# Adaptive-norm modulation vectors: row sums on VectorE from transposed weights instead of column sums closed by TensorE

## Chip, cores and metric

One core of one Trainium2 chip runs the whole program. The metric is the device time of one execution in microseconds (us); the time of a kernel is the median of several runs. The engines are named as in the profile: PE is TensorE (PEld its weight loads), DVE is VectorE, ACT is ScalarE, POOL is GpSimd, and SP issues most of the DMA transfers.

## The reference

Two layers over 256 tokens of width 2048: an RWKV-7 time mix with an MLP, then a chunked band attention with an MLP. Each sub-layer is modulated by vectors that come from the conditioning vector `c` alone:

```python
for layer in range(DEPTH):                      # DEPTH = 2, D = 2048
    mod = c @ w_ada[layer] + b_ada[layer]       # (1, D) @ (D, 6 * D)
    sh1, sc1, gt1, sh2, sc2, gt2 = jnp.split(mod, 6, axis=-1)
    if layer == N_A_LAYERS:
        sh_kv, sc_kv = jnp.split(c @ w_ada_kv + b_ada_kv, 2, axis=-1)
        ...
    h = modulate(rms_norm(x, g_mix[layer]), sh1, sc1)
    ...
    x = x + gt1[:, None, :] * y
    h = modulate(rms_norm(x, g_mlp[layer]), sh2, sc2)
    x = x + gt2[:, None, :] * sq_relu_mlp(h, w_up[layer], w_down[layer])
```

So there are 14 modulation vectors of 2048 numbers, each a product of `c` with a 2048x2048 matrix of 16 MB in fp32. The change concerns the last twelve of them, in the order in which the kernel makes them: gate, scale, shift and gate of layer 0, the two of the shared key and value projection, and the six of layer 1.

## The kernel before

Activations lie transposed: a tile has 128 channels on its partitions and the 256 tokens along the row. A vector over channels lies as `[128, 16]`, channel `128*k + p` at partition `p`, column `k`. Every dense product runs in a split form: a weight tile `raw` of 128x1024 (512 KB, 4 KB for each partition) is loaded by SP, ScalarE rounds it to `wH` (`halves`, L378), VectorE forms the rest `wL = raw - wH` (L381), and TensorE multiplies both (`proj2`, L412 and L413). `raw` has six buffers, `wH` and `wL` three each.

The stages follow each other: the opening (to about 190 us) makes the first two modulation vectors and the value projection; then the recurrence of layer 0, 16 pairs of heads in a software pipeline of slots, beside the dense projections for the next pairs (`layer_a`, to about 680 us); its output projection (`out_proj`); the first MLP (`mlp`, four quarters of 16 up and 16 down tiles); the shared key and value projections and attention (`attention`); its output projection; and the second MLP. The order of instructions on each engine is a scheduler's; the program text gives the dependencies.

The twelve later modulation vectors are made in small steps between other work. `ada_tiles` lists the weight tiles: for each vector two halves of 1024 output columns, for each half 16 tiles of 128 rows. `ada_load` loads the next one (as `raw`, or as `rada` out of a pool of its own during the MLPs and attention), and `ada_step` takes one tile: `acc += c[row of the partition] * tile` on VectorE (L452 for the first tile of a half, L454 for the other fifteen), with `acc` a tile of 128x1024. Who calls it: one step in three of four slots of the recurrence, `ada_tick` with one or two steps for each MLP tile, one or two steps for each projection in attention, and `ada_need`, which makes what is still missing of a vector just before its use.

After the sixteenth tile of a half, `acc` holds for each of 1024 columns 128 partial sums, one on each partition. `ada_sum` adds them on TensorE: for each of 8 blocks of 128 columns and each group of 32 columns a matmul with `acc` as the stationary operand and a column of ones as the moving one, which leaves the sums spread over partitions in PSUM (L476); VectorE adds the bias into the vector `mods[key]` (L480). `fin` runs the generator to its end at once, since `lazy` is never set. The profile shows each of these fp32 matmuls as two.

Of the kernel before, what the change touches and what calls it, by code (L numbers as in the profile page):

```python
# [329 lines left out]
class Body:  # L330
# [88 lines left out]

    def ada_src(self, layer, part):  # L420
        if layer == "kv":
            at, w = 2 * 96 + 16 * part, self.d["w_ada_kv"]
        else:
            at, w = 96 * layer + 16 * part, self.d["w_ada"][layer]
        return w[:, part * D:(part + 1) * D], self.bada[:, at:at + KT]

    def ada_tiles(self):
        for key in [(0, 2), (0, 4), (0, 3), (0, 5), ("kv", 1), ("kv", 0),
                    (1, 1), (1, 0), (1, 2), (1, 4), (1, 3), (1, 5)]:
            for half in range(KT // HK):  # L430
                for kt in range(KT):
                    yield key, half, kt

    def ada_load(self):
        tile_ = next(self.adas, None)
        if tile_ is not None:
            key, half, kt = tile_
            w, n_ = self.ada_src(*key)[0], HK * P
            raw = self.raw(w[kt * P:(kt + 1) * P, half * n_:(half + 1) * n_], ada=True)
            self.ada_q.append((key, half, kt, raw))  # L440
        return tile_ is not None

    def ada_step(self):
        nc = self.nc
        if not (self.ada_q or self.ada_load()):
            return
        key, half, kt, raw = self.ada_q.popleft()
        ck = self.ct[:, kt:kt + 1]
        if kt == 0:
            self.fin(HK)  # L450
            self.acc = self.wp.tile([P, HK * P], F32, tag="acc", bufs=1, name="acc")
            nc.vector.tensor_scalar(out=self.acc, in0=raw, scalar1=ck, scalar2=0.0, op0=ALU.mult, op1=ALU.add)  # L452
        else:
            nc.vector.scalar_tensor_tensor(out=self.acc, in0=raw, scalar=ck, in1=self.acc, op0=ALU.mult, op1=ALU.add)  # L454
# [11 lines left out]
    def ada_drain(self, n):  # L466

        for _ in range(min(n, len(self.ada_q))):
            self.ada_step()

    def ada_sum(self, acc, dst, half, bias):
        nc = self.nc
        ps = self.psm()[:, :HK]
        for n in range(HK):
            for g in range(0, P, 32):
                nc.tensor.matmul(ps[g:g + 32, n:n + 1], acc[:, n * P + g:n * P + g + 32], self.col(C_ONE),  # L476
                                 start=True, stop=True, tile_position=(0, g))
# [5 lines left out]
    def fin(self, n):  # L483
        for _ in range(n):
            next(self.fins, None)

    def ada(self, n=1):
        for _ in range(n):
# [7 lines left out]
    def ada_need(self, *keys):  # L496
        while not all(k in self.ada_done for k in keys):
            self.ada_step()
        self.fin(HK)

    def gain(self, g, key):
        t = self.gp.tile([P, KT], F32, name=f"gain_{g}")
# [70 lines left out]
    def run(self):  # L573
        nc, tc, d = self.nc, self.tc, self.d
        ctx = self.ctx
        gp = self.gp = ctx.enter_context(tc.tile_pool(name="gp", bufs=1))
        self.wp = ctx.enter_context(tc.tile_pool(name="wp", bufs=2))
        nc.scalar.preload_act_table_set("natural_log_exp_and_others")
        self.hp = ctx.enter_context(tc.tile_pool(name="hp", bufs=2))
        self.csts = gp.tile([P, CST.shape[1]], F32, name="csts")  # L580
        self.vecs = gp.tile([P, len(VECS), KT], F32, name="vecs")
        self.bada = gp.tile([P, 2 * 96 + 32], F32, name="bada")
        self.ct = gp.tile([P, KT], F32, name="ct")
        nc.scalar.dma_start(out=self.ct, in_=d["c"])
# [5 lines left out]
        self.lazy, self.fins, self.ada_pool = False, iter(()), None  # L590
        self.ada_done = set()
        self.adas, self.ada_q = self.ada_tiles(), deque()

        sv, sp = ExitStack(), ExitStack()
        v = self.layer_a(sv, sp)
        with ExitStack() as st:
            self.np = st.enter_context(tc.tile_pool(name="npl", bufs=1, side="right", reuse_waits="tile"))
            xp = st.enter_context(tc.tile_pool(name="xp", bufs=1, side="right", reuse_waits="tile"))
            self.x = xp.tile([P, KT, T], F32, name="x")
            for j in range(KT - 2, KT):  # L600
                self.split(self.y_hl, j, v[:, j, :])
            sv.close()
            self.ada_need((0, 2), (0, 4), (0, 3))
            nxt = self.out_proj(self.pp, "w_o", self.y_hl, (0, 2), "g_mlp0", (0, 4), (0, 3), self.o_ps)
            sp.close()
            with ExitStack() as s2:
                pp = s2.enter_context(tc.tile_pool(name="ps_m0", bufs=2, space=bass.MemoryType.PSUM, reuse_waits="tile"))
                self.psm = lambda: pp.tile([P, 512], F32, tag="m", bufs=2, name="m")
                s2.enter_context(self.ada_room(5))
                nxt = self.mlp(s2, pp, 0, *nxt, "g_kv", ("kv", 1), ("kv", 0))  # L610
            with ExitStack() as s2:
                pp = s2.enter_context(tc.tile_pool(name="ps_at", bufs=2, space=bass.MemoryType.PSUM, reuse_waits="tile"))
                self.psm = lambda: pp.tile([P, 512], F32, tag="m", bufs=1, name="m")
                s2.enter_context(self.ada_room(3))
                o_hl = self.attention(s2, pp, *nxt)
                self.ada_need((1, 2), (1, 4), (1, 3))
                nxt = self.out_proj(pp, "attn_w_o", o_hl, (1, 2), "g_mlp1", (1, 4), (1, 3))
            with ExitStack() as s2:
                pp = s2.enter_context(tc.tile_pool(name="ps_m1", bufs=2, space=bass.MemoryType.PSUM, reuse_waits="tile"))
                self.psm = lambda: pp.tile([P, 512], F32, tag="m", bufs=2, name="m")  # L620
                s2.enter_context(self.ada_room(5))
                self.mlp(s2, pp, 1, *nxt)
                r = self.rstd()
                for lo, hi, eng in ((0, 4, nc.vector), (11, 14, nc.gpsimd), (4, 8, nc.vector), (8, 11, nc.vector),
                                    (14, KT, nc.gpsimd)):
                    x = self.x[:, lo:hi, :]
                    eng.tensor_tensor(out=x, in0=x, in1=r.unsqueeze(1).to_broadcast([P, hi - lo, T]), op=ALU.mult)  # L627
                    (nc.sync if eng is nc.vector else nc.scalar).dma_start(out=d["out"][:, lo:hi, :], in_=x)

    def layer_a(self, st, sp):  # L630
# [6 lines left out]
        with ExitStack() as s1:  # L637
# [22 lines left out]
            def ada_blocks():  # L660
# [3 lines left out]
                for w_ in blocks:  # L664
                    W, ks = w_ * P, 8 // w_
                    ps = self.psm().rearrange("p (i n) -> p i n", i=2)
                    for part in (1, 0):
                        w, _ = self.ada_src(0, part)
                        w = w[:, lo * P:lo * P + W].rearrange("(a i p) n -> a p i n", p=P, i=ks)
                        for a in range(KT // ks):  # L670
                            raw = pb.tile([P, HK * P], F32, tag="rawa", bufs=6, name="rawa")
                            raw = raw.rearrange("p (i n) -> p i n", i=ks)
# [31 lines left out]
                                                 start=True, stop=True, tile_position=(0, g))  # L704
                    o = slice(lo, lo + w_)
                    for part in (1, 0):
                        bias = self.ada_src(0, part)[1]
# [107 lines left out]
        with ExitStack() as s1:  # L815
# [55 lines left out]
            for slot in range(S * NPAIR + Pair.STEPS):  # L871
# [28 lines left out]
            self.fin(HK)  # L900
        return v

    def out_proj(self, pp, wname, hl, gate, g, sc, sh, begun=()):
# [241 lines left out]
def _arrange(x, c, w_ada, b_ada, g_mix, g_mlp, w_up, w_down,  # L1145
# [3 lines left out]
             attn_w_q, attn_w_o, attn_rel_bias,  # L1149
             w_ada_kv, b_ada_kv, g_kv, w_k_shared, w_v_shared, g_final):  # L1150
    f = lambda a: np.ascontiguousarray(np.asarray(a))
    x, mu = f(x), f(rwkv_mu)[0]
    g_mix, g_mlp = f(g_mix), f(g_mlp)
    vecs = [g_mix[0], g_mix[1], g_mlp[0], g_mlp[1], f(g_kv), f(g_final)] + [mu[i] for i in range(6)] + [
# [6 lines left out]
    for i, w in ((0, rwkv_w2), (1, rwkv_a2)):  # L1161
# [45 lines left out]
```

## Time and profile before

| what | before |
|---|---|
| median of 3 runs | 2672.63 us (2672.55 to 2673.03) |
| the profiled execution, whole | 2673.81 us |
| its span | 2672.0 us |
| data moved by DMA | 662.64 MB, mean 248 GB/s |
| granted TensorE clock, mean | 0.994 of full speed |

In the profile's groups a row names the line, engine and operation, the tiles (out<-in), shapes, count, then busy us in all, mean ns of one, and the idle time of the engine before them with what ended it. The table of stretches gives, for each stretch of time, its length, the busy us and count of each engine, the granted clock, the share of the DMA engines and GB/s. A wait names who waited for whom, us in total, times, and the longest. A timeline row has start, duration, engine, line, operation and tiles. A DMA row has the tile and tensor, count, KB and the median us from issue to landing.

### The profile page before, as it was taken

To read this page: it belongs to the slowest core of one execution; us is meant where nothing else is said; L and a number is where in the kernel's file an instruction comes from. 1 tells how busy PE (TensorE), PEld (TensorE's weight loads), DVE (VectorE), ACT (ScalarE), POOL (GpSimd) and SP (SyncE) were. 2 spreads that over 40 slices of the span, in tenths; PEclk is the share of its full clock that TensorE was granted. 3 is DMA by queue.
4 is the path that set the end of the run, shared out by engine and by line. 5 is a ranking of instruction groups with operands and counts; after the bars stand their busy time and mean duration, and the time that the engine had idled before them with its cause. 6 is when DMAs were issued, how large, how long until landed. Compare 5 with 4: busy or idle time off the path is not lost. (4 is left out here: it accounts for less than half of the span.)

```text
span 2672.0 us, 58365 instructions
## 1 busy us (share of the span) xinstructions
PE 2600.1 (97%) x23690; PEld 2225.4 (83%) x23690; DVE 2101.0 (79%) x3109; ACT 1343.9 (50%) x2432; POOL 209.7 (8%) x320
## 2 busy tenths in 40 slices
PE   6999999999999999999999999999999999999997
PEld 3777788788899888888888998877898888888886
DVE  5778888889789888888888898899887556555555
ACT  3345555555456445355365554565564463453554
POOL 0001322332110000000000100000100000000002
PEclk9999999999999999999999999999999999999999
DMA  9966556565768888899898679887766555555553
GB/s 337 314 236 211 192 173 210 189 206 195 245 240 304 324 309 321 322 324 331 320 328 294 238 240 325 324 274 259 264 216 237 186 187 188 189 186 185 189 189 119
DMA packets 217390, 662.64 MB, mean 248 GB/s; under 512 B 21408, under 2 KB 68896, under 8 KB 217120
## 3 DMA queue, kind: packets, MB, share of 16 engines
q1 hardware_dynamic: 215056, 656.36, 71.1%
q8 instruction: 186, 3.05, 0.5%
q10 hardware_dynamic: 2064, 2.54, 0.3%
q14 instruction: 84, 0.69, 0.1%
HBM read 656.72 MB, written 2.10 MB: 247 GB/s over the span
## 5 line engine op out<-in xcount | busy, mean ns | idle before, releaser
L381 DVE TENSOR_TENSOR wL<-raw,wH 128x1024 fp32r<-128x1024 f32 x772 | 940.9, 1220 | 342.6 <-ACT wH L378 337.8
L378 ACT CAST wH<-raw 128x1024 fp32r<-128x1024 f32 x772 | 805.5, 1045 | 801.2 <-PE pj L412 646.0
L412 PE MATMUL pj<-aHL,wH 128*128 128x512 f32 x3328 | 1201.9, 403 | 2.0 <-DVE x L927 1.1
L413 PE MATMUL pj<-aHL,wL 128*128 128x256 f32 x3328 | 936.3, 281 | 0.0
L412 PEld LDWEIGHTS pj<-aHL,wH 128*128 128x128 f32 x3328 | 629.5, 189 | 154.1 <-issue 9.2
L412 PE MATMUL pj<-hHL,wH 128*128 128x512 f32 x2048 | 724.6, 399 | 0.0
L413 PEld LDWEIGHTS pj<-aHL,wL 128*128 128x128 f32 x3328 | 629.7, 189 | 2.6 <-issue 0.8
L413 PE MATMUL pj<-hHL,wL 128*128 128x256 f32 x2048 | 574.7, 281 | 0.0
L412 PEld LDWEIGHTS pj<-hHL,wH 128*128 128x128 f32 x2048 | 384.8, 188 | 95.7 <-DVE hHL L973 0.2
L413 PEld LDWEIGHTS pj<-hHL,wL 128*128 128x128 f32 x2048 | 387.0, 189 | 0.1
L454 DVE SCALAR_TENSOR_TENSOR acc<-rada,ct,acc 128x1024 f32<-128x1024 f32 x256 | 327.5, 1279 | 8.4 <-DMA rada<-w_ada 7.5
L518 POOL TENSOR_TENSOR ss<-ss,sq 128x256 f32<-128x256 f32 x56 | 54.5, 974 | 1590.8 <-ACT sq L517 1590.5
L998 DVE SCALAR_TENSOR_TENSOR x<-pj,mod,x 128x256 f32<-128x256 f32 x256 | 123.3, 482 | 59.5 <-PE pj L413 55.7
L454 DVE SCALAR_TENSOR_TENSOR acc<-raw,ct,acc 128x1024 f32<-128x1024 f32 x104 | 136.4, 1312 | 15.5 <-DMA raw<-w_ada 15.4
L401 PE MATMUL pj<-aHL,wH 128*128 128x258 f32 x384 | 109.0, 284 | 0.0
L402 PE MATMUL pj<-aHL,wH 128*128 128x258 f32 x384 | 109.0, 284 | 0.0
L970 ACT ACTIVATE t<-t 128x256 f32<-128x256 f32 x112 | 46.8, 418 | 122.6 <-DVE t L942 122.6
L403 PE MATMUL pj<-aHL,wL 128*128 128x258 f32 x384 | 108.0, 281 | 0.0
L403 PEld LDWEIGHTS pj<-aHL,wL 128*128 128x128 f32 x384 | 73.2, 191 | 0.2
L402 PEld LDWEIGHTS pj<-aHL,wH 128*128 128x128 f32 x384 | 72.6, 189 | 0.1
L401 PEld LDWEIGHTS pj<-aHL,wH 128*128 128x128 f32 x384 | 72.2, 188 | 0.2
L972 ACT ACTIVATE t<-t 128x256 f32<-128x256 f32 x128 | 53.4, 417 | 3.4
(244 smaller groups left out, 2812.3 us busy)
## 6 DMA issues: line engine op xcount, KB each, us to landing
raw<-w_up SPq DMA_DIRECT2D x256, 512.0 KB, 4.1
raw<-w_down SPq DMA_DIRECT2D x256, 512.0 KB, 4.1
rada<-w_ada SPq DMA_DIRECT2D x209, 512.0 KB, 5.7
raw<-w_ada SPq DMA_DIRECT2D x111, 512.0 KB, 4.4
rawa<-w_ada SPq DMA_DIRECT2D x64, 512.0 KB, 6.8
rada<-w_ada_kv SPq DMA_DIRECT2D x64, 512.0 KB, 6.6
raw<-w_k SPq DMA_DIRECT2D x32, 512.0 KB, 4.2
raw<-w_r SPq DMA_DIRECT2D x32, 512.0 KB, 4.5
```

Of the source, the lines that this page charges most:

```text
L378: nc.scalar.copy(Hf, raw)
L381: eng.tensor_tensor(out=Lf, in0=raw, in1=Hf, op=ALU.subtract)
L401: nc.tensor.matmul(ps, H[:, i, :], a(kt)[:, 0, :], start=(first and kt == 0), stop=False)
L402: nc.tensor.matmul(ps, H[:, i, :], a(kt)[:, 1, :], start=False, stop=False)
L403: ins = nc.tensor.matmul(ps, L[:, i, :], a(kt)[:, 0, :], start=False, stop=(last and kt == KT - 1))
L412: nc.tensor.matmul(ps, H[:, i, :], a(kt), start=(kt == 0), stop=False)
L413: ins = nc.tensor.matmul(ps[:, 0, :], L[:, i, :], a(kt)[:, 0, :], start=False, stop=(kt == KT - 1))
L454: nc.vector.scalar_tensor_tensor(out=self.acc, in0=raw, scalar=ck, in1=self.acc, op0=ALU.mult, op1=ALU.add)
L518: (eng or nc.gpsimd).tensor_tensor(out=self.ss, in0=self.ss, in1=sq, op=ALU.add)
L970: nc.scalar.activation(t, t, AF.Relu)
L972: nc.scalar.activation(t, t, AF.Square)
L998: nc.vector.scalar_tensor_tensor(out=x, in0=ps[:, i, :], scalar=self.mods[(layer, 5)][:, n:n + 1], in1=x, op0=ALU.mult, op1=ALU.add)
```

## The change

The host hands in the weights of the twelve vectors transposed, as `w_ada_t`: 192 blocks of 128 output channels, each as two tiles of 128x1024, one for each half of the 2048 inputs, every tile in one contiguous piece. The first two vectors' weights of layer 0 stay as they were, in an array of their own, `w_ada0` (2048x4096). `c` is handed in a second time as a row, `c_row`.

A step now multiplies a tile, whose partitions are output channels, with `cb`, half of `c` repeated on every partition, and the instruction's accumulator output writes the row's sum into one column: into `sums` for the first half of the inputs, into the vector itself for the second. After sixteen tiles the bias is added to `sums`, `c_half` loads the other half of `c` into `cb` (one buffer, 512 KB), and after the next sixteen `sums` is added to the vector. The half that was used last for one vector is used first for the next, so `cb` is loaded once at the start and once for each vector. The product itself is written over the weight tile. `ada_sum`, `fin`, `lazy` and the tile `acc` are gone. The count of steps, 384, and who calls them stay the same.

```diff
+    def c_half(self):
+        n_ = HK * P
+        self.cb = self.wp.tile([P, n_], F32, tag="cb", bufs=1, name="cb")
+        self.nc.sync.dma_start(out=self.cb, in_=self.d["c_row"][0:1, self.cb_half * n_:(self.cb_half + 1) * n_].to_broadcast([P, n_]))
+        self.cb_half = 1 - self.cb_half
...
-        key, half, kt, raw = self.ada_q.popleft()
-        ck = self.ct[:, kt:kt + 1]
-        if kt == 0:
-            self.fin(HK)
-            self.acc = self.wp.tile([P, HK * P], F32, tag="acc", bufs=1, name="acc")
-            nc.vector.tensor_scalar(out=self.acc, in0=raw, scalar1=ck, scalar2=0.0, op0=ALU.mult, op1=ALU.add)
+        key, last, n, raw = self.ada_q.popleft()
+        if self.cb is None:
+            self.c_half()
+        dst, bias = self.mods[key], self.ada_src(*key)[1]
+        sums = dst if last else self.sums
+        nc.vector.scalar_tensor_tensor(out=raw, in0=raw, scalar=1.0, in1=self.cb, op0=ALU.mult, op1=ALU.mult,
+                                       accum_out=sums[:, n:n + 1])
+        if n < KT - 1:
+            return
+        if last:
+            nc.vector.tensor_tensor(out=dst, in0=dst, in1=self.sums, op=ALU.add)
+            self.ada_done.add(key)
         else:
-            nc.vector.scalar_tensor_tensor(out=self.acc, in0=raw, scalar=ck, in1=self.acc, op0=ALU.mult, op1=ALU.add)
-        if kt == KT - 1:
-            self.fins = self.ada_sum(self.acc, self.mods[key], half, self.ada_src(*key)[1])
-            if not self.lazy:
-                self.fin(HK)
-            if half == KT // HK - 1:
-                self.ada_done.add(key)
+            nc.vector.tensor_tensor(out=self.sums, in0=self.sums, in1=bias, op=ALU.add)
+            self.c_half()
...
-    def ada_sum(self, acc, dst, half, bias):
-        nc = self.nc
-        ps = self.psm()[:, :HK]
-        for n in range(HK):
-            for g in range(0, P, 32):
-                nc.tensor.matmul(ps[g:g + 32, n:n + 1], acc[:, n * P + g:n * P + g + 32], self.col(C_ONE),
-                                 start=True, stop=True, tile_position=(0, g))
-            if n == HK - 1:
-                o = slice(half * HK, (half + 1) * HK)
-                nc.vector.tensor_tensor(out=dst[:, o], in0=ps, in1=bias[:, o], op=ALU.add)
-            yield
...
-        "w_ada": f(w_ada), "w_ada_kv": f(w_ada_kv),
+        "w_ada0": f(w_ada[0][:, :2 * D]), "c_row": f(c).reshape(1, D),
+        "w_ada_t": f(np.concatenate([w.T for w in (w_ada[0][:, 2 * D:], w_ada[1], np.asarray(w_ada_kv))], 0)
+                     .reshape(12 * KT, P, 2, HK * P).transpose(0, 2, 1, 3)),
```

More of the change, by code (lines that the diff above doesn't have):

```diff
@@ L421, in ada_src @@
         if layer == "kv":
-            at, w = 2 * 96 + 16 * part, self.d["w_ada_kv"]
+            at, tile_ = 2 * 96 + 16 * part, KT * (10 + part)
         else:
-            at, w = 96 * layer + 16 * part, self.d["w_ada"][layer]
-        return w[:, part * D:(part + 1) * D], self.bada[:, at:at + KT]
+            at, tile_ = 96 * layer + 16 * part, KT * (6 * layer + part - 2)
+        return tile_, self.bada[:, at:at + KT]
     def ada_tiles(self):
@@ L429, in ada_tiles @@
                     (1, 1), (1, 0), (1, 2), (1, 4), (1, 3), (1, 5)]:
-            for half in range(KT // HK):
-                for kt in range(KT):
-                    yield key, half, kt
+            for last in range(2):
+                for n in range(KT):
+                    yield key, last, n
     def ada_load(self):
@@ L436, in ada_load @@
         if tile_ is not None:
[L437 to L440, printed above, removed]
-        return tile_ is not None
+            key, last, n = tile_
+            if n == 0 and last:
+                self.half = 1 - self.half
+            raw = self.raw(self.d["w_ada_t"][self.ada_src(*key)[0] + n, self.half], ada=True)
+            self.ada_q.append((key, last, n, raw))
+        return tile_ is not None
+    def c_half(self):
[3 more added lines that the diff above has]
+        self.cb_half = 1 - self.cb_half
     def ada_step(self):
@@ L469, in ada_drain @@
             self.ada_step()
-    def ada_sum(self, acc, dst, half, bias):
-        nc = self.nc
-        ps = self.psm()[:, :HK]
-        for n in range(HK):
-            for g in range(0, P, 32):
-                nc.tensor.matmul(ps[g:g + 32, n:n + 1], acc[:, n * P + g:n * P + g + 32], self.col(C_ONE),
-                                 start=True, stop=True, tile_position=(0, g))
-            if n == HK - 1:
-                o = slice(half * HK, (half + 1) * HK)
-                nc.vector.tensor_tensor(out=dst[:, o], in0=ps, in1=bias[:, o], op=ALU.add)
-            yield
-    def fin(self, n):
-        for _ in range(n):
-            next(self.fins, None)
     def ada(self, n=1):
@@ L589, in run @@
         self.nhalf, self.pool_every = 0, 0
-        self.lazy, self.fins, self.ada_pool = False, iter(()), None
+        self.ada_pool, self.half, self.cb, self.cb_half = None, 0, None, 0
+        self.sums = gp.tile([P, KT], F32, name="ada_sums")
         self.ada_done = set()
@@ L706, in ada_blocks @@
                     for part in (1, 0):
[L707 removed]
+                        bias = self.bada[:, KT * part:KT * part + KT]
                         nc.vector.tensor_tensor(out=self.mods[(0, part)][:, o], in0=ps[:, 2 * part:2 * part + w_],
@@ L1151, in _arrange @@
     f = lambda a: np.ascontiguousarray(np.asarray(a))
+    w_ada = f(w_ada)
     x, mu = f(x), f(rwkv_mu)[0]
```

5 lines of the change are left out of this document (1 added, 4 removed).

## The prediction

> **What bounds the kernel now.** I read the page's busy shares first, then a table of busy time over stretches cut where the work changes (opening, first layer's recurrence, its output projection, first MLP with its tail, second half, attention, second MLP), then the waits.
>
> ```profile
> span 2672.0 us, 58365 instructions
> PE 2600.1 (97%) x23690; PEld 2225.4 (83%) x23690; DVE 2101.0 (79%) x3109; ACT 1343.9 (50%) x2432; POOL 209.7 (8%) x320
> ```
> ```profile
> core 0: us, PE busy (x) PEld busy (x) DVE busy (x) ACT busy (x) POOL busy (x), PEclk, DMA share, GB/s
> 230.00:680.00 450.00, 430.78 (x8996) 354.87 (x8996) 387.66 (x728) 235.06 (x659) 124.52 (x169) 0.99 0.60 194
> 680.00:800.00 120.00, 116.33 (x1007) 105.48 (x1004) 99.81 (x142) 62.04 (x111) 15.12 (x18) 0.99 0.75 257
> 800.00:1279.00 479.00, 479.00 (x3270) 419.66 (x3269) 421.54 (x498) 239.94 (x351) 0.00 (x0) 1.00 0.88 320
> 1279.00:1700.00 421.00, 420.44 (x2880) 371.78 (x2879) 363.38 (x452) 213.51 (x314) 14.29 (x24) 1.00 0.82 291
> 1700.00:1840.00 140.00, 139.34 (x990) 108.34 (x989) 129.14 (x278) 83.16 (x217) 6.38 (x54) 1.00 0.82 282
> 1840.00:2030.00 190.00, 188.69 (x1311) 168.94 (x1310) 168.40 (x233) 107.55 (x174) 13.11 (x14) 1.00 0.73 255
> ```
> ```profile
> ACT wH L378 <- PE pj L412: 646.0, 448, 4.3
> DVE wL L381 <- ACT wH L378: 337.8, 280, 2.0
> ```
>
> TensorE sets the end: between 800 and 2030 us it is busy for all but a few us, and in the recurrence (230 to 680) for 431 of 450. The waits say the same from the other side: ScalarE waits 646 us for TensorE to give back a weight buffer, and VectorE waits for ScalarE. VectorE is second, and not far off: 88% busy in the first MLP, 92% in attention. So time taken from TensorE's queue shortens the run, as long as VectorE stays under the line.
>
> **What is removed.** Each of the 24 half vectors ended with a burst of small matmuls that summed `acc` over partitions. The price is their time in TensorE's queue.
>
> ```profile
> L476 PE MATMUL m<-csts,acc 128*32 128x1 f32 x1152 | 13.2, 172 | 0.0
> L476 PE MATMUL ms<-csts,acc 128*32 128x1 f32 x384 | 4.3, 172 | 0.0
> ```
> ```profile
> 1633.27 0.40 PE L412 MATMUL pj<-aHL,wH 128*128 128x512 f32 x1
> 1633.50 0.28 PE L413 MATMUL pj<-aHL,wL 128*128 128x256 f32 x1
> 1633.62 0.39 PE L412 MATMUL pj<-aHL,wH 128*128 128x512 f32 x1
> 1633.85 0.28 PE L413 MATMUL pj<-aHL,wL 128*128 128x256 f32 x1
> 1634.06 0.71 PE L476 MATMUL m<-csts,acc 128*32 128x1 f32 x64
> 1634.70 0.50 PE L412 MATMUL pj<-aHL,wH 128*128 128x512 f32 x1
> 1635.04 0.28 PE L413 MATMUL pj<-aHL,wL 128*128 128x256 f32 x1
> 1635.16 0.40 PE L412 MATMUL pj<-aHL,wH 128*128 128x512 f32 x1
> ```
>
> 1152 + 384 = 1536 matmuls of 64 to a burst are 24 bursts: 18 in the later stages (`m`), 6 in the recurrence (`ms`). The busy column, 17.5 us, is too little. A pair of large matmuls starts every 0.35 us (1633.27 to 1633.62). Without the burst the next two pairs would start at 1633.97 and 1634.32; they start at 1634.70 and 1635.16. The burst therefore costs 0.84 us: its issue, the gap in front and the slow first matmul behind it (0.50 us). 18 x 0.84 = 15.1 us. In the recurrence TensorE is 96% busy (430.78 of 450), so I let 96% of 6 x 0.84 count: 4.8 us. Removed from the path: 20 us.
>
> **What VectorE gets.** The same 384 tiles of 128x1024 are multiplied, in three ways dearer.
>
> ```profile
> L381 DVE TENSOR_TENSOR wL<-raw,wH 128x1024 fp32r<-128x1024 f32 x772 | 940.9, 1220 | 342.6 <-ACT wH L378 337.8 <-PE o L403 0.4
> L454 DVE SCALAR_TENSOR_TENSOR acc<-rada,ct,acc 128x1024 f32<-128x1024 f32 x256 | 327.5, 1279 | 8.4 <-DMA rada<-w_ada 7.5
> L452 DVE TENSOR_SCALAR acc<-rada,ct 128x1024 f32<-128x1024 f32 x17 | 12.7, 744 | 0.0
> L1087 ACT ACTIVATION_READ_ACCUMULATOR s<-s,mx 128x1 f32 x64 | 12.0, 187 | 0.0
> L823 DVE MEMSET e<- 128x4 f32 x2 | 0.1, 62 | 0.0
> L145 DVE TENSOR_TENSOR_SCAN s<-csts,s 128x256 f32<-128x256 f32 x16 | 11.3, 707 | 0.0
> L166 DVE SCALAR_TENSOR_TENSOR s<-k,vecs,s 128x256 f32<-128x256 f32 x16 | 7.6, 476 | 0.0
> L1086 DVE TENSOR_REDUCE mx<-s 128x1 f32<-128x128 f32 x64 | 18.9, 342 | 0.2
> ```
>
> First, 24 of them were one-source multiplies (744 ns) and become two-source: 24 x (1279 - 744) = 12.8 us. Second, the row sum must be read out. No VectorE row of before sums beside a product; ScalarE's does, and its profile holds a second instruction of 187 ns. The cheapest VectorE instruction here, a write without input, takes 62 ns. I bound the read-out by 62 and 187 ns and take 100, nearer the first since it too only writes: 38 us of VectorE in all. Third, the product itself might run slower while it sums. Below: TENSOR_REDUCE carries a sum along the row, and its 342 ns are for rows of 128 and 256 (mean 192), against 476 for a 256-element product, so a running sum need not slow an element; that end is 1279 ns. Above: the scan, which also carries a value along the row, takes 707 where the product takes 476, 0.90 ns more per element; for 1024 elements 0.92 us more. I take the lower end, because the reduction is an add, as here, and the scan a multiply and an add. The 24 small adds at the ends of the halves are replaced by 24 others, and nothing changes there.
>
> Does VectorE have room? These are the old products by stage; each burst stands for one multiply more, of the one-source kind (L452).
>
> ```profile
> core 0: us, DVE busy (x), PEclk, DMA share, GB/s
> 230.00:680.00 450.00, 118.59 (x90) 0.99 0.60 194
> 680.00:800.00 120.00, 19.13 (x15) 0.99 0.75 257
> 800.00:1279.00 479.00, 151.79 (x119) 1.00 0.88 320
> 1279.00:1700.00 421.00, 106.37 (x84) 1.00 0.82 291
> 1700.00:1840.00 140.00, 30.57 (x24) 1.00 0.82 282
> 1840.00:2030.00 190.00, 37.50 (x29) 1.00 0.73 255
> ```
>
> First MLP: 119 + 8 products. Idle VectorE is 479 - 421.5 = 57.5 us, less 6.7 that the stage gets shorter (8 x 0.84), less 8 x 0.535 = 4.3: 46.5 us, or 0.37 us for each product. Attention (1700 to 1840), 24 + 2: 140 - 129.1 - 1.7 - 1.1 = 8.1 us, 0.31 us each. Recurrence, 90 + 6: 62.3 - 4.8 - 3.2 = 54 us, 0.57 us each. At 0.1 or 0.19 us the extra is covered by that idle time everywhere; the cover is gone at 0.31 us in attention and 0.37 in the MLP. Not quite free: in the recurrence and in attention TensorE waits for chains that pass through VectorE. The recurrence has 19.2 us of TensorE idle; if idle grows with VectorE's load (9.6 + 3.2 on 388, 3%), that is 0.6 us; I put 2 us for both stages, from 0 to 6 (all 19.2 us growing by a third).
>
> The Trainium skill has a rule against this change: "Vector Engine (DVE) Microarchitecture Reference", section "Points that are easy to get wrong", says that a scalar-tensor-tensor with two sources in SBUF that are not bf16 runs at half throughput, with no read port left for the accumulator. Read so that the halving comes on top of today's price, it would give the time of the second rival, about 2850 us. The trace agrees only with one half of it: the two-source form takes 1279 ns against 744 for one source, a price that the kernel pays already.
>
> **The reloaded row of c.** `cb` holds half of c on every partition, 512 KB, loaded once and then once per vector, 13 loads. It has one buffer, so a reload starts only after the sixteenth product, and the seventeenth waits for it on VectorE; queued behind that are the `wL` subtractions, which TensorE needs, and the adds that give PSUM banks back. In the order of the changed kernel the scheduler has put some ten VectorE instructions between the two products, five or six in two attention reloads. On SP's queue the load stands, in the MLP, behind a weight load that waits for a later VectorE instruction anyway, so nothing new is held there. Nothing of before loads one row to all partitions; the nearest rows are loads of its size:
>
> ```profile
> raw<-w_up SPq DMA_DIRECT2D x96, 512.0 KB, 6.5
> raw<-w_down SPq DMA_DIRECT2D x86, 512.0 KB, 7.3
> csts<-cst ACTq DMA_DIRECT2D x1, 480.0 KB, 10.2
> ```
> ```profile
> 1005.03 1.05 ACT L378 CAST wH<-raw 128x1024 fp32r<-128x1024 f32 x1 [1.74 <-PE pj L412]
> 1007.31 1.21 DVE L381 TENSOR_TENSOR wL<-raw,wH 128x1024 fp32r<-128x1024 f32 x1
> ```
>
> The first two are medians inside the first MLP (745 to 1279), the third the slowest load of this size. Between issue and the waiting product lie about two half weights, each 8 x 0.35 = 2.8 us of TensorE, so 5.6 us. A landing of 6.5 to 7.3 us makes VectorE wait 1 to 1.7 us. The slack behind it: a cast starts when TensorE gives back a buffer of three, so TensorE wants the new one two half weights later, 1005.03 + 5.6 = 1010.6; its `wL` is done at 1008.5. That is 2.1 us of cover, and the wait disappears in it. At 10.2 us the wait is 4.6, of which 2.5 show: 12 x 2.5 = 30 us. I take 2 us for the two short reloads in attention; bounds 0 and 30. Where cover is gone, `wL` is late next.
>
> The opening reads its weights from a narrower array with the same packet size; I take 0. Other bytes: 13 x 0.5 MB, 1% more, on a share of 0.88 at most: 0.
>
> **Sum.** -15.1 - 4.8 + 2 (chains) + 2 (reloads) = -16 us. The profiled execution took 2673.81 us, its span of 2672.0 and 1.8 around it; it would take 2657.8. The median of the runs is 1.2 us lower, 2672.63, so the forecast is 2656.6.
>
> **Rivals.**
> 1. *The reload is late.* If sixteen engines that read the same 4 KB slow each other, it lands at 10 us or later and TensorE waits for `wL` once a vector: -20 + 2 + 30 = +12, 2685 us. For it: nothing like it has been run here, and VectorE has only 2.1 us of cover. Against: 4 KB packets as for every weight, and the scheduler's distance.
> 2. *VectorE becomes the bound (slower).* It decides when a product costs more than the 0.31 to 0.37 us of room. At the scan's price, 0.92 + 0.10 us each, VectorE's load goes to 387.7 + 96 x 1.02 + 3.2 = 489 us in the recurrence's 450, and in the same way to 555 in 479, 458 in 421, 157 in 140 and 200 in 190 (from 680 to 800 us it still fits, 117 in 120): 39 + 76 + 37 + 17 + 10 = 179 us over, 2852 us. For it: the scan's row. Against: the reduction's.
> 3. *The gain doesn't arrive.* A read-out of 187 ns with the drain around it, say 0.27 us, leaves VectorE above 95% in the MLP and attention; each wait for it then reaches TensorE, and the freed 20 us go to such waits. 2664 to 2676 us. For it: attention's 0.31 us. Against: the three weight buffers between the two engines.
> 4. *Everything hidden*, -20 or a little more: 2648 to 2652 us.
>
> **How the numbers follow.** Forecast, 2652 to 2664: 0.56. Rival 4: 0.08. Rival 3: 0.13, of which 0.03 is still faster by over 0.2%. Rival 1: 0.10. Rival 2: 0.13, one row of a carried value against another. About 0.2%, 5.3 us, is what a measurement of this kernel can tell from no change. Faster: 0.56 + 0.08 + 0.03 = 0.67; within: 0.09 of rival 3, 0.01 of rival 1: 0.10; slower: 0.23. The range leaves out rival 2 and a little: 2648 to 2692.
>
> **What would show it.** Right: no L476 matmuls, TensorE still over 99% busy from 800 to 2030, and that stretch with the recurrence shorter by about 20 us; the new product at 1.28 us with a second instruction of 0.06 to 0.19 us; VectorE about 50 us busier. Wrong: a product of 2 us; waits of VectorE for `c_row` over 3 us, with TensorE idle behind them; or an opening whose length to 190 us has changed.

## The result, and the profile after

The changed kernel is slower. Its median is 2743.77 us (2742.68 to 2750.59, four runs) against 2672.59 us (2672.17 to 2673.03, four runs) for the kernel before on the same chip: a ratio of 1.027, 95% interval 1.0257 to 1.0282, or about 71 us. The forecast was 2656.6 us and the range ended at 2692. The profiled execution has a span of 2741.5 us (2672.0 before), at a mean granted clock of 0.989 (0.994 before).

From the page of the changed kernel: the span, the busy shares, and the chain of work that ended last, by engine and then by line.

```profile
span 2741.5 us, 55497 instructions
PE 2611.7 (95%) x22154; PEld 2220.0 (81%) x22154; DVE 2093.3 (76%) x3493; ACT 1333.7 (49%) x2432; POOL 199.4 (7%) x320
PE 59%; DMA 17%; DVE 14%; issue 6%; ACT 2%; SPq 0%; POOL 0%; DVEq 0%; ACTq 0%; POOLq 0%
PE pj L412 31%; PE pj L413 16%; DMA rada<-w_ada_t 10%; DVE wL L381 6%; DMA raw<-w_ada_t 5%; DVE raw L459 2%; DVE rada L459 2%; PE pj L403 1%; PE pj L401 1%; PE pj L402 1%; ACT wH L378 1%; DMA raw<-w_up 1%; PE ms L324 1%; DVE mix L723 0%; PE iv L111 0%
```

No engine has become the bound by its load: TensorE went down from 97% to 95%, VectorE from 79% to 76%. The chain names something else: the loads of the transposed weights (`rada`, `raw` from `w_ada_t`) stand on it with 15%, and the products and `wL` on VectorE behind them. (That is a share of the chain, not time lost.)

The chain of the kernel before holds no transfer, but it can't be set beside this one: its shares add up to 39%, for it is followed back only to 1620 us, behind the first MLP. So the comparison below goes by stages and waits.

```profile
PE 38%; DVE 1%; issue 0%; DVEq 0%; ACT 0%; ACTq 0%
```

Where the time lies, in us, with the stages cut at the same instructions of both traces (the first and the last transpose `tt` of the recurrence, the first and the last `aHL` made with `gain_g_mlp`, and the first `ks`):

| stage | before | after | difference |
|---|---|---|---|
| opening | 243.9 | 245.7 | +1.8 |
| recurrence of layer 0 | 441.7 | 455.6 | +13.9 |
| its output projection | 36.9 | 34.9 | -2.0 |
| first MLP and its tail | 798.5 | 856.5 | +58.0 |
| key and value projections, attention | 414.1 | 414.7 | +0.6 |
| second MLP (no modulation work) | 736.9 | 734.1 | -2.8 |

The first MLP carries most of it. The tables of busy time by stretch, before and then after, each from the start of its first MLP to the end of its last quarter:

```profile
core 0: us, PE busy (x) PEld busy (x) DVE busy (x) ACT busy (x) POOL busy (x), PEclk, DMA share, GB/s
723.00:1431.00 708.00, 708.00 (x4821) 622.95 (x4820) 614.57 (x737) 361.89 (x537) 12.97 (x14) 1.00 0.86 312
```
```profile
736.00:1486.00 750.00, 716.25 (x4119) 621.69 (x4120) 614.30 (x912) 354.87 (x537) 12.31 (x14) 0.99 0.86 302
```

Before, TensorE had no idle time in these 708 us. After, it does 702 instructions less (11 bursts of 64 with two records missing, at 0.84 us some 9 us of its queue), VectorE is busy for the same 614 us, the share of the DMA engines is the same, and yet TensorE idles for 33.75 us, and it is busy for 716.25 us, more than the 699 or so that its remaining work took before. (Its granted clock is 0.99 there, 1.00 before.) The waits say for whom. After, in order of VectorE's waits and of TensorE's:

```profile
engine line waited for: us in total, times, longest us
DVE rada L459 <- DMA rada<-w_ada_t: 114.4, 98, 4.5
DVE raw L459 <- DMA raw<-w_ada_t: 29.3, 32, 2.6
DVE rada L459 <- DMA cb<-c_row: 6.1, 4, 2.6
PEld pj L413 <- DVE wL L381: 38.4, 58, 2.4
PE pj L413 <- DVE wL L381: 20.8, 30, 2.0
```

and the same pair of waits on VectorE before:

```profile
DVE acc L454 <- DMA raw<-w_ada: 15.4, 15, 2.0
DVE acc L454 <- DMA rada<-w_ada: 7.5, 13, 1.2
```

The wait that I had priced, for the reload of `c_row`, is 6.1 us in all. The wait that I had not priced is for the product's own weights: 144 us in 130 waits, against 23 in 28.

One such wait, followed through three engines. SP first (start, duration; a DMA that waits for its buffer isn't issued until it is free), then VectorE, then TensorE, all in the changed kernel's timeline:

```profile
998.06 3.00 SPq L368 DMA_DIRECT2D raw<-w_up  x2
1001.11 0.42 SPq L368 DMA_DIRECT2D rada<-w_ada_t  x1
```
```profile
999.48 1.22 DVE L381 TENSOR_TENSOR wL<-raw,wH 128x1024 fp32r<-128x1024 f32 x1
1000.84 1.22 DVE L459 SCALAR_TENSOR_TENSOR rada<-rada,cb 128x1024 f32<-128x1024 f32 x1
1001.99 0.08 DVE L459 DVE_READ_ACCUMULATOR rada<-rada,cb 128x1 f32 x1
1001.99 1.22 DVE L381 TENSOR_TENSOR wL<-raw,wH 128x1024 fp32r<-128x1024 f32 x1
...
1004.98 1.23 DVE L381 TENSOR_TENSOR wL<-raw,wH 128x1024 fp32r<-128x1024 f32 x1 [1.43 <-ACT wH L378]
...
1008.56 1.23 DVE L459 SCALAR_TENSOR_TENSOR rada<-rada,cb 128x1024 f32<-128x1024 f32 x1 [2.03 <-DMA rada<-w_ada_t]
1009.71 0.08 DVE L459 DVE_READ_ACCUMULATOR rada<-rada,cb 128x1 f32 x1
1009.71 1.22 DVE L381 TENSOR_TENSOR wL<-raw,wH 128x1024 fp32r<-128x1024 f32 x1
```
```profile
1009.18 0.39 PE L412 MATMUL pj<-aHL,wH 128*128 128x512 f32 x1
1010.99 0.39 PE L413 MATMUL pj<-aHL,wL 128*128 128x256 f32 x1 [1.42 <-DVE wL L381]
```

The `wL` that starts at 999.48 ends at 1000.70 and gives a `raw` buffer back. Only then can SP issue the second of the two weight loads (the pair ends at 1001.06), and the product's load, which stands behind them on SP, goes out at 1001.11. Matched one to one with the issues, it is the load that the product at 1008.56 waits for, 7.45 us later (the loads of `rada` around it take 6.1 to 7.5 us from issue to landing). VectorE has two `wL` and small work for that time, then idles 2.03 us; the next `wL` is late, and TensorE waits 1.42 us for it. And as a late `wL` gives its `raw` buffer back late, SP reaches the next load of a product late too.

Did the loads slow down, or were they issued too late? Before, a load of `rada` took 5.7 us (209 of them) and 6.6 us (64) in the median; after, 6.3. The time from a load's issue to its product fell much more: from 12.45 us in the median to 7.09. So they were issued too late. What SP waited for in the first MLP (the two stretches above) shows the turn; before, then after:

```profile
SPq L368 <- DVE acc L454: 198.7, 113, 4.2
SPq L368 <- DVE wL L381: 137.1, 82, 5.6
```
```profile
SPq L368 <- DVE wL L381: 338.7, 153, 6.5
...
SPq L368 <- DVE rada L459: 3.0, 2, 1.9
```

Before, SP stood there 113 times, 199 us, at a buffer that a product had still to give back, so SP was up with the room that the products gave back. After, it does so twice, for 3 us; it stands at weight loads (339 us), with the products' loads queued behind. The Trainium skill, "DMA: Bandwidth & Descriptors", section "Anatomy of one DMA — SWDGE (gpsimd) path", says that DMA engines don't wait for semaphores: the wait is made by the sequencer that issues, ahead of the dispatch. The section is about issues from GpSimd; for SP the timeline above agrees: the `rada` load, whose own buffer had been free for over 5 us, leaves 0.41 us after the `wL` of another tile.

### The profile page after: what moved, and what is told of

The parts are those of the page before. It is cut to its first block, busy times and chain, and to the rows that moved or that the text cites. A ratio compares the mean times of both kernels' runs of the same rounds, so it can differ in the third digit from the quotient of the medians.

```text
span 2741.5 us, 55497 instructions
## 1 busy us (share of the span) xinstructions
PE 2611.7 (95%) x22154; PEld 2220.0 (81%) x22154; DVE 2093.3 (76%) x3493; ACT 1333.7 (49%) x2432; POOL 199.4 (7%) x320
## 4 chain that ended last, share of the span: by engine, by line
PE 59%; DMA 17%; DVE 14%; issue 6%; ACT 2%; SPq 0%; POOL 0%; DVEq 0%; ACTq 0%; POOLq 0%
PE pj L412 31%; PE pj L413 16%; DMA rada<-w_ada_t 10%; DVE wL L381 6%; DMA raw<-w_ada_t 5%; DVE raw L459 2%; DVE rada L459 2%; PE pj L403 1%; PE pj L401 1%; PE pj L402 1%; ACT wH L378 1%; DMA raw<-w_up 1%; PE ms L324 1%; DVE mix L723 0%; PE iv L111 0%
## 5 line engine op out<-in xcount | busy, mean ns | idle before, releaser
L459 DVE SCALAR_TENSOR_TENSOR rada<-rada,cb 128x1024 f32<-128x1024 f32 x273 | 333.2, 1223 | 130.9 <-DMA rada<-w_ada_t 114.4
L459 DVE SCALAR_TENSOR_TENSOR raw<-raw,cb 128x1024 f32<-128x1024 f32 x111 | 137.9, 1247 | 29.9 <-DMA raw<-w_ada_t 29.3
L960 ACT ACTIVATE t<-t 128x256 f32<-128x256 f32 x112 | 47.0, 420 | 221.5 <-DVE t L932 221.5
L961 ACT ACTIVATE hHL<-t 128x256 fp32r<-128x256 f32 x128 | 53.0, 414 | 5.0 <-DVE t L556 4.5
```

The lines of the kernel that those rows point to most:

```text
L459: nc.vector.scalar_tensor_tensor(out=raw, in0=raw, scalar=1.0, in1=self.cb, op0=ALU.mult, op1=ALU.mult, accum_out=sums[:, n:n + 1])
L960: nc.scalar.activation(t, t, AF.Relu)
L961: nc.scalar.activation(h[:, 0, :], t, AF.Square)
```

## The theories

The two traces show the same from the other side. For a load of `rada`, count the `wL` that VectorE runs between the load's issue on SP and the product that uses it. Before the change there are 6.6 in the mean, after it 2.9, and 185 of the 273 loads have exactly 2. Two half weights are 5.6 us of TensorE, which is less than a landing.

Theory L (load order): the scheduler sets the order of every engine from its own model of time. Before, there was a tie between TensorE and the products: `acc` has one buffer, so the first product of the next half had to wait until the burst had read it, and with that the scheduler kept the products at TensorE's pace and their loads well ahead. Without the tie it places products earlier on VectorE and their loads, against them, later on SP.

Against it stood four rivals: the product with its read-out is dear; the reload of `c`; the transposed, contiguous weights load otherwise; and the length of the bursts, which had given the loads time to land.

## The experiments

All ratios are against the kernel before on the same chip, with a 95% interval. The last two columns are VectorE's wait for `rada` loads in the profile, and the mean count of `wL` between issue and use, as above, in that kernel's trace.

| kernel | median us | ratio | wait for `rada`, us | `wL` ahead |
|---|---|---|---|---|
| before | 2672.6 | 1 | 7.5 | 6.6 |
| after | 2743.8 | 1.0270 (1.0257 to 1.0282) | 114.4 | 2.9 |
| e1, before without the burst | 2756.7 | 1.0297 (1.0278 to 1.0317) | 145.0 | 2.5 |
| e2, after, loads in program order | 2688.9 | 1.0055 (1.0039 to 1.0072) | 24.6 | 4.4 |
| e5, after with a tie | 2688.7 | 1.0057 (1.0042 to 1.0072) | 10.9 | 6.2 |
| e6, after with bursts that tie nothing | 2750.3 | 1.0285 (1.0268 to 1.0301) | 129.7 | 2.7 |
| e7, e1 with a tie | 2658.7 | 0.9951 (0.9934 to 0.9968) | 8.7 | 6.6 |
| e11, e5 without the reload | 2672.9 | 0.9997 (0.9988 to 1.0007) | 8.1 | 6.5 |
| e13, both halves in a tile | 2668.1 | 0.9979 (0.9970 to 0.9988) | 8.1 | 6.5 |

**e1: the kernel before, only TensorE's burst taken out.** The sum over partitions is left out: the bias is added to the first eight columns of `acc` as they are, so this kernel and e7, which is built on it, don't make the modulation vectors.

```diff
-        ps = self.psm()[:, :HK]
+        ps = acc[:, :HK]
         for n in range(HK):
-            for g in range(0, P, 32):
-                nc.tensor.matmul(ps[g:g + 32, n:n + 1], acc[:, n * P + g:n * P + g + 32], self.col(C_ONE),
-                                 start=True, stop=True, tile_position=(0, g))
```

> The kernel before with the sum over partitions left out (the bias is added to the first eight columns of acc as they are), nothing else: row-major weights, no accumulator output, no reload of c. In the order that results on SP the load of a modulation tile stands about four weight loads later against its product than before, as in the changed kernel. Theory L (the loads were moved late by the scheduler once TensorE's part was gone, VectorE waits for them): slower than before, 2715 to 2750 us, with over 80 us of VectorE waiting for rada. Rival V (the new product, its read-out or the reload of c costs the time): these are absent and TensorE's 20 us are saved, so 2648 to 2660 us.

Measured 2756.71 us, ratio 1.0297, slower by a little more than expected. VectorE's waits in this kernel (6 us more for `rada` loads stand at L452):

```profile
DVE acc L454 <- DMA rada<-w_ada: 101.3, 96, 2.8
DVE acc L454 <- DMA rada<-w_ada_kv: 37.7, 40, 2.0
DVE acc L454 <- DMA raw<-w_ada: 27.6, 30, 2.4
```

This kernel has no transposed weights, no read-out and no reload; it only does less on TensorE, and it is slower by about as much as the changed one, with the same waits. The product, the reload and the layout are out as the main cause.

**e2, e3, e4: the products' loads held in program order on SP.** In e2, the changed kernel keeps the loads of the modulation weights and the dense weights in the order of the program text during the MLPs and attention. e3 does so in the recurrence and in the output projection too. e4 is the kernel before with e2's edit.

```diff
-        self.nc.sync.dma_start(out=t, in_=src)
+        ins = self.nc.sync.dma_start(out=t, in_=src)
+        if self.ada_pool:
+            self.tc.keep_in_program_order(ins)
```

> The changed kernel with the loads of raw and rada held in program order on SP during the MLPs and attention; the recurrence is left as it is. Theory L: the 55 us lost between 700 and 1700 us come back and TensorE's saving shows there, the recurrence keeps its 16 us: 2660 to 2680 us, VectorE's wait for rada under 20 us. Rival V: the product and the reload are unchanged, so 2730 to 2750 us.

> As e2, with the recurrence's loads held in program order as well. Theory L: the recurrence's 16 us come back too, 2645 to 2665 us, faster than both kernels. Rival V: 2730 to 2750 us. If the recurrence is lost for another reason than the load order, it equals e2.

> The kernel before with the loads of raw and rada held in program order during the MLPs and attention. Theory L: its loads are early already, so no gain: 2665 to 2680 us. If program order is simply a better order for any kernel, it is faster by as much as e2 is against the changed kernel.

e2: 2688.85 us; e3: 2686.22 us, ratio 1.0043 (1.0030 to 1.0056). Nothing but the order has changed, and some 55 of 71 us are back. Both stay above what I expected (2660 to 2680 and 2645 to 2665). In e3's profile the recurrence takes 434.9 us against 453.3 in e2, but the output projection (48.6 against 35.5) and the first MLP with its tail (805.2 against 797.2) take the gain back. e4 missed what I expected by far: 2755.05 us, ratio 1.0298 (1.0280 to 1.0315). Its waits on ScalarE, and one of SP's (L454 is the first product of a half in this kernel):

```profile
ACT wH L380 <- DMA raw<-w_down: 66.3, 27, 9.1
ACT wH L380 <- DMA raw<-w_up: 21.0, 13, 6.0
```
```profile
SPq L368 <- DVE acc L454: 185.4, 15, 18.6
```

Here the order harms from the other side: a product's load that waits for its own buffer (up to 18.6 us) stands ahead of a dense weight, and now the dense weight is late. So program order isn't better in itself; what counts is that neither kind of load stands behind one that has to wait longer.

**e5, e6, e7: the tie alone.** e5 gives the changed kernel one small matmul for each half vector, whose result nobody uses, but which reads a tile that is written next (`cb` by the reload, `sums` by the next vector's products). e6 gives it the bursts back (32 matmuls in the program, 64 in the profile), on the last weight tile; no later product waits for them, only a small copy of their result that nobody uses. e7 is e1 with one small matmul that reads `acc`.

In e5:

```diff
         if n < KT - 1:
             return
+        ps = self.psm()[:, :HK]
+        src = self.sums if last else self.cb[:, :KT]
+        nc.tensor.matmul(ps[0:KT, 0:1], src, self.col(C_ONE), start=True, stop=True)
```

In e6, at the same place:

```diff
+        ps = self.psm()[:, :HK]
+        for m in range(HK):
+            for g in range(0, P, 32):
+                nc.tensor.matmul(ps[g:g + 32, m:m + 1], raw[:, m * P + g:m * P + g + 32], self.col(C_ONE),
+                                 start=True, stop=True, tile_position=(0, g))
+        nc.vector.tensor_copy(self.ct[:, :HK], ps)
```

In e7, on top of e1, in `ada_sum`:

```diff
+        nc.tensor.matmul(self.psm()[0:32, 0:1], acc[:, 0:32], self.col(C_ONE), start=True, stop=True)
         ps = acc[:, :HK]
```

> The changed kernel with one small matmul behind each half, which reads cb after the first half and sums after the second, its result unused: the next half's products must again wait until TensorE has come so far, as they had to for the buffer of acc. Theory T (the tether: without that wait the scheduler runs the products ahead of TensorE's pace and puts their loads late): the order of loads before returns by itself, nothing is pinned, and TensorE's 20 us are saved less 24 small matmuls: 2650 to 2665 us, VectorE's wait for rada under 30 us. Rival B (the length of the bursts sets the order): still 2735 to 2750 us.

> The changed kernel with the bursts put back, 64 matmuls for each half with the last weight tile as the stationary operand, their result unused; nothing that VectorE does next waits for them. Theory T: the loads stay late and TensorE has its 20 us again, 2745 to 2775 us. Rival B: the order of before returns, 2670 to 2685 us.

> As e1, the kernel before with its sum over partitions left out, but with one small matmul that reads acc at the end of each half. No accumulator output, no reload of c. Theory T: the loads return to their places, 2648 to 2662 us against 2757 in e1; the difference to e5 is what product, read-out and reload cost. Rival B: like e1, 2740 to 2760 us.

e5: 2688.66 us; e6: 2750.33 us; e7: 2658.68 us. VectorE's waits, of e5 and then of e6, and the first MLP of e7 in the table of stretches:

```profile
DVE rada L459 <- DMA rada<-w_ada_t: 10.9, 13, 3.3
```
```profile
DVE rada L459 <- DMA rada<-w_ada_t: 129.7, 120, 3.3
```
```profile
726.00:1426.00 700.00, 698.61 (x4135) 614.42 (x4135) 612.15 (x738) 362.33 (x538) 12.91 (x14) 1.00 0.86 313
```

The bursts without the tie bring nothing back; the tie without the bursts does. That leaves theory L. SP's waits in the first MLP of e5 (740 to 1448 us) say it directly:

```profile
SPq L368 <- DVE wL L381: 243.9, 157, 5.6
SPq L368 <- DVE rada L459: 157.0, 89, 13.3
```

With no order set by hand, SP again stands at buffers that products give back, 89 times, against twice in the changed kernel. Between e1 and e7 there are 24 tiny matmuls and some 92 us by the ratios. e7's row also answers the prediction's first step: with the bursts gone and the loads on time, TensorE is busy 698.61 of 700 us, and the stage is 8 us shorter than before (708). e5 came back only by 55 us, less than I expected, so something else in the changed kernel costs the rest.

**e8, e9, e10: order by hand in further stages.** e8 is e5 with the loads of the recurrence in program order; e9 is the changed kernel, without a tie, with those of the recurrence and of the first MLP; e10 is e9 with the tie. The first two lines are in all three, the setting around the MLP in e9 and e10; a load is held in order where `in_order` is set:

```diff
+                self.in_order = slot < S * NPAIR
                 if slot < S * NPAIR:
...
+                self.in_order = True
                 nxt = self.mlp(s2, pp, 0, *nxt, "g_kv", ("kv", 1), ("kv", 0))
+                self.in_order = False
```

> e5 with the loads of the recurrence alone held in program order (as in e3, but not those of the output projection). If what is left in e5 is the recurrence's load order (456 us there, 435 in e3, 442 before), the stages add up to 2694 - 21 = 2673 us in the profile, about 2668 by median, the same as before or a little faster. If it is the product or the reload, e8 stays at e5's 2689.

> The changed kernel without the small matmuls, the loads of the recurrence and of the first MLP held in program order and nothing else. From the stages of earlier runs: recurrence 435 (e3), first MLP 698 (e2), attention as in the changed kernel: about 2660 us, faster than before by 0.3 to 0.6%.

> e9 with the small matmuls of e5: the first MLP at 698 us as in e2 and the start of attention without the 7 us that e2 lost there: 2650 to 2660 us, the fastest. If the reload behind the small matmul costs more than the order gains, slower than e9.

2684.34 (ratio 1.0051), 2678.76 (1.0024) and 2692.96 us (1.0079). All three stayed above what I expected. e8's recurrence took 445.7 us against 455.9 in e5, but most of that was not seen at the end. The tie and the order by hand don't add up: e10 is slower than e9, as the alternative in its expectation had it, though nothing here shows that the reload is the reason.

**e11: is it the reload?** As e5, but `c` is loaded once and both halves of the weights are multiplied with its first half.

```diff
-            self.c_half()
...
-        src = self.sums if last else self.cb[:, :KT]
+        src = self.sums
```

> As e5, but c is loaded once and never again: both halves of a vector are multiplied with the first half of c and summed into sums, so the second half of c is left out. The 384 products, their accumulator read-outs, the transposed weights and a small matmul behind each half stay, and the loads then stand where they stand in e7. If the 30 us between e5 and e7 are the reload (the wait for its data, and the products and loads that it moves), 2655 to 2668 us. If they are the product with its read-out, 2680 to 2695 us as e5.

2672.85 us, between the two times expected; ratio 0.9997 against e5's 1.0057: the reload and its tie cost 0.6%, 16 us. In e5 the reload waits for the small matmul as well, which the changed kernel doesn't ask of it, so for the changed kernel this is an estimate.

**e12, e13: no reload, and all of the computation.** A tile holds 64 output channels: their first 1024 inputs on partitions 0 to 63, the other 1024 on 64 to 127. `cb` holds both halves of `c` the same way, for the whole run. After 16 products two matmuls with two identity blocks, one above the other, add the two halves of a channel and lay 1024 results out as the vector needs them. These matmuls read `sums`, so they are the tie as well. e13 adds the recurrence's order of e8.

```diff
-            nc.vector.tensor_tensor(out=self.sums, in0=self.sums, in1=bias, op=ALU.add)
-            self.c_half()
+        pairs = self.sums.rearrange("p (k i) -> p i k", i=2)
+        for i in range(2):
+            nc.tensor.matmul(ps[C * i:C * i + C, :], self.cst("eye"), pairs[:, i, :], start=True, stop=True)
+        o = slice(half * HK, (half + 1) * HK)
+        nc.vector.tensor_tensor(out=dst[:, o], in0=ps, in1=bias[:, o], op=ALU.add)
```

> A version of the change without reload and with a natural tie to TensorE: a weight tile holds 64 output channels, one half of the inputs on the lower and the other on the upper 64 partitions, cb holds both halves of c for good, and after sixteen products two matmuls with a stacked identity add the two halves of each sum. Loads stand where they stand in e7 and e11. If order and reload are all that was lost, it equals e11, 2665 to 2677 us, 65 to 80 us under the changed kernel; if the reload matters less than e11 against e5 says, it stays near 2689.

> e12 with the recurrence's loads held in program order as in e8, which took 10 us from the recurrence there. If what e11 lost against e7 (12 us by median, 5 of it in the recurrence's stage) is again where loads stand, 2655 to 2668 us; if it is the product's own cost, as e12.

e12: 2674.30 us, ratio 1.0003 (0.9994 to 1.0012), the same as e11, which bears the price of the reload out. e13: 2668.07 us, ratio 0.9979 (0.9970 to 0.9988): about 5 us faster than the kernel before and 76 faster than the changed one, at the upper end of what was expected. VectorE's waits for products' loads in e13 are as short as they were before the change:

```profile
DVE raw L458 <- DMA raw<-w_ada_t: 9.4, 13, 1.3
DVE rada L458 <- DMA rada<-w_ada_t: 8.1, 11, 1.7
```

## Why the prediction was wrong

The sum, in shares of 2673 us from the ratios; each has some 5 us on either side:

| step | from | us |
|---|---|---|
| TensorE's bursts gone, tie kept | e7 against before | -13 |
| transposed product with its read-out, in place of the chain on `acc` | e11 against e7 | +12 |
| reload of `c` | e5 against e11 | +16 |
| tie gone: products' loads late | after against e5 | +57 |
| all | after against before | +72 |

The tie's share does not lie in the recurrence: in the profiles that stage takes 455.9 us in e5, as in the changed kernel (455.6), and 447.9 in e11, without the reload.

- **The step that failed** is the one under the reloaded row, "On SP's queue the load stands, in the MLP, behind a weight load that waits for a later VectorE instruction anyway, so nothing new is held there", with the words above it, "The same 384 tiles of 128x1024 are multiplied". I looked at where the new load stands and took the place of the 384 old ones, against their products, as unchanged, so the sum has no term for their waits. That place had moved: for the loads of `rada` from 6.6 `wL` ahead to 2.9. It cost 57 us of the 72. None of the four rivals named it; rival 1 was a late load, but of `c_row`, and VectorE waits for the reloads 6.1 us in all. Nor does one of the three signs of being wrong that I had named show: the product takes 1.22 us, the longest wait for `c_row` is 2.6 us, and the opening is 1.8 us longer.
- **What is removed: right in kind, somewhat too large.** Forecast 20 us, measured 13 (interval of e7: 9 to 18), with 24 tiny matmuls left in.
- **The product: cheaper than forecast.** After:

```profile
L459 DVE SCALAR_TENSOR_TENSOR rada<-rada,cb 128x1024 f32<-128x1024 f32 x273 | 333.2, 1223 | 130.9 <-DMA rada<-w_ada_t 114.4 <-DMA cb<-c_row 6.1 <-DMA raw<-w_up 3.9
L459 DVE DVE_READ_ACCUMULATOR rada<-rada,cb 128x1 f32 x273 | 22.5, 83 | 0.0
```

  The multiplication takes 1223 ns, the read-out 83 ns (bounds 62 and 187, taken 100), together 1306 ns against 1279 for the old product. But they overlap: in the timeline above the read-out and the next instruction both start at 1001.99, 1.15 us behind the product, and over all `rada` products with no wait behind them the median from start to next start is 1.15 us, against 1.20 before. VectorE's busy time did not rise by 50 us; it fell from 2101.0 to 2093.3. So rival 2 falls: no cost of the sum along the row shows. Choosing the lower end was partly luck: the reason given, that the reduction at L1086 is an add, misreads the kernel, where it is a maximum (`op=ALU.max`). That an instruction with an accumulator output is two instructions is what the Trainium skill says in "VectorE: DVE Perf Modes", section "Two Vector instructions with no wait between them"; the two rows agree. The halving that the Trainium skill states in the "Vector Engine (DVE) Microarchitecture Reference", section "Points that are easy to get wrong", read as coming on top, is not borne out: 1223 ns with the sum, 1279 without it. (Worked through like rival 2, with 1.28 us more for each product and 0.10 for the read-out, that reading would have given, as an estimate, some 2990 us, not the 2850 of the prediction.)
- **The cover on VectorE: the sum of busy time was right and the conclusion wrong.** I had 46.5 us of idle time for the products in the first MLP, and VectorE's load did fit. But idle time in a sum doesn't say when a tile arrives: the waits for products' loads, 144 us over the run, stand ahead of `wL`, where the waits for a cast had stood.
- **The reload: mis-sized.** Taken at 2 us, with 30 as the upper bound; e5 against e11 shows 16. Its landing was forecast well: 6.5 to 7.3 us by the loads of the same size, and the row of the changed kernel says

```profile
cb<-c_row SPq DMA_DIRECT2D x13, 512.0 KB, 6.3
```

  The 6.1 us of VectorE's direct waits for it are far below 16; where the rest arises (the reload's place in the order, or e5's small matmul ahead of it) was not separated.
- **The opening: right.** Up to the first `tt` it takes 245.7 us, 243.9 before.
- **The 12 us between e7 and e11 were not split up.** The recurrence takes 443.3 us in e7 and 447.9 in e11; its order by hand gives about 6 us back (e13 against e12). The rest is open, as is the reason why e10's two remedies disturb each other.

That the scheduler's order comes from the lost tie is shown by e5 and e7 against e6 and e1. How its model of time arrives at just that order is only argued.

## What to carry to other kernels

When an edit takes an engine out of a chain, look for the waits that go with it: a tile with a single buffer can be what keeps a producer, and the loads ahead of it, at the pace of the slowest engine. With a scheduler in between, compare the order of each DMA queue with the order of the engine that uses its loads, load by load, and turn the distance into time: here two half weights, 5.6 us, were less than a landing of 6.3 us. One dependent instruction that computes nothing can be worth 2 to 4% (e5, e7).

## What was not expected of the hardware

- A VectorE product of two fp32 sources with a running sum takes 1223 ns for 128x1024, 56 ns less than the same instruction with a second tile as its output and no sum (1279 ns); the read-out is 83 ns. Which of the differences (output over its own input, constant in place of a column as the scalar, the sum) makes it faster was not tried.
- A load of one 4 KB row to all 128 partitions lands in 6.3 us in the median, the same as the 512 KB loads of `rada` beside it, 6.3 us. All partitions reading the same bytes cost nothing that the rows show.
